# The up projection of two channel mixers: tokens stationary instead of weights, with the result turned back through 32x32 blocks and DRAM

## The chip, the cores and the metric

The kernel runs on one core of a Trainium2 chip. Five engines work side by side on it: TensorE (PE in the profile, its weight loads on a row of their own, PEld), VectorE (DVE), ScalarE (ACT), GpSimd (POOL) and SyncE (SP). Each takes its instructions strictly in the order of its own queue. Data moves between DRAM and the on-chip memory through 16 DMA engines that all queues share. Here SP issues nearly all transfers. The metric is device time in microseconds of one execution; the median of three runs stands for the kernel.

## The reference, cut to what matters

Two layers work on 256 tokens with 2048 features, all in float32. Layer 0 mixes tokens with gated linear attention, layer 1 with forgetting attention, and each also attends to 256 memory tokens. After each mixer comes a channel mixer, and this is where the change lies:

```python
def causal_dwconv(u, w, b):
    s_ = u.shape[1]
    up = jnp.pad(u, ((0, 0), (CONV_WIDTH - 1, 0), (0, 0)))
    return w[0] * up[:, 0:s_] + w[1] * up[:, 1:s_ + 1] + w[2] * up[:, 2:s_ + 2] + b

def conv_ffn(h, w_up, conv_w, conv_b, w_down):
    u = causal_dwconv(h @ w_up, conv_w, conv_b)
    a, val = split_cols(u, [FFN_HIDDEN, FFN_HIDDEN])
    return (jax.nn.silu(a) * val) @ w_down
```

`h` is the normalised residual (256 x 2048), `w_up` is 2048 x 11264 (a gate half and a value half of 5632 columns each), `w_down` is 5632 x 2048. The convolution runs along the tokens, with its own three weights and a bias for every hidden column.

## The kernel before

**Precision.** A float32 product is made from parts. Every activation and every weight is split into a rounded high part and the remainder (`hi`, `lo`), and a product is hi·hi + lo·hi + hi·lo. The weights stream from DRAM as units of 128 x 1024 values (512 KB, `raw`, four buffers). ScalarE rounds a unit to `whi` (L199, three buffers), VectorE subtracts to get `wlo` (L208, three buffers). So every unit passes SP, ScalarE and VectorE before TensorE can use it, and its `whi` buffer is free again when TensorE has used the unit up.

**Two forms of a projection.** `proj_fm` (L211 on) keeps a 128 x 128 block of weights stationary and streams the tokens. One matmul takes the weights' high part against both parts of the activations side by side (512 columns, L233 and L236), a second the weights' low part against the high part of the activations (256 columns, L234). The result has features on partitions and tokens along the row; the two halves of the 512 columns are added afterwards by `whole` (a copy on ScalarE, L241, and an addition on VectorE, L243). A unit holds four chunks of 128 input features by 256 output columns. `proj_tm` (L246 on) keeps 128 tokens stationary and streams 512 weight columns, three matmuls for each chunk of input features and each half of the tokens (L270, L271, L272). Its result has tokens on partitions. A unit holds two chunks by 512 columns.

**The channel mixer.** `ffn` (L780 on) goes through the hidden columns in three parts of 16, 16 and 12 blocks of 128 (`PARTS`). For each block `j` an up panel by `proj_fm` gives 128 gate columns and the 128 value columns that belong to them. Each result is put together by `whole`, multiplied by the norm's row of token factors into a tile `u` with two leading zeros (L795), convolved along the row (one ACTIVATE at L799, two VectorE operations at L800 and L801), and the pair of results goes through SiLU (L804), the product (L805) and `split` (L296, L297) into the tile of high and low parts that the down projection reads. After each part, four down panels by `proj_tm` add into the residual (L774). There are 44 up panels and 12 down panels in each layer. The first down panel of a part reads the part's blocks in order, two for each unit, so it needs the last two blocks only with its last unit: the eighth unit in a part of 16, the sixth in the part of 12.

**What sets the order of the work.** A planner (the tile scheduler) fixes each engine's queue at build time. It plays the program on a modelled machine and gives an engine, whenever that is free, the first in program order of the instructions whose inputs are there in the model; the weight stream (`split_unit`) has its place in that order moved ahead by 300. On the chip the queues then run in exactly that order, with semaphores for the dependencies. The accumulators in PSUM have four banks, and an up panel takes two of them, so a panel can be computed while the one before is read out.

The functions that the change touches, and what calls them:

Of the kernel before, what the change touches and what calls it, by code (L numbers as in the profile page):

```python
# [39 lines left out]

OG_EARLY = 2
# [13 lines left out]
def _panels():  # L55
# [79 lines left out]
M_N = M_LVL + NVER * len(LEVELS)  # L135
# [3 lines left out]
def _trunk(ctx: ExitStack, tc: tile.TileContext, xt, xtok, memt, wp, wgu, gns, gfin, cnv, par, msk, out):  # L139
# [12 lines left out]
    mask = const.tile([P, M_N], F32, name="mask")  # L152
# [15 lines left out]
    mk = [const.tile([P, MEM_H, T], F32, name=f"mk{l}") for l in range(2)]  # L168
    mv = [const.tile([P, 2, MEM_H * HD], F32, name=f"mv{l}") for l in range(2)]
# [76 lines left out]
    def proj_tm(key, src, evac, spare=None):  # L246

        units = where[key]  # L250
        n = units[0][2]
        base = min(min(u[1]) for u in units)
        acc = [pacc.tile([P, 512], F32, name="acc", tag="acc") for _ in range(2)]
        ahead = 0 if spare is None else 4
        ready = {}
        for i in range(len(units) + ahead):
            for b, u in ((0, i), (1, i - ahead)):
                if not 0 <= u < len(units):
                    continue
# [5 lines left out]
                xs = slice(b * P, (b + 1) * P)  # L265
                for j, kc in enumerate(kcs):
                    s = slice(j * n, (j + 1) * n)
                    xk = src[kc - base]
                    last = u == len(units) - 1 and j == len(kcs) - 1
                    TE.matmul(a, xk[:, 0, xs], hi[:, s], start=u == 0 and j == 0, stop=False)  # L270
                    TE.matmul(a, xk[:, 0, xs], lo[:, s], start=False, stop=False)  # L271
                    TE.matmul(a, xk[:, 1, xs], hi[:, s], start=False, stop=last)  # L272
                if u == len(units) - 1:
                    evac(b, a)
# [27 lines left out]
    class Norm:  # L302


        def __init__(self, n, tag="x"):
            self.n, self.tag = n, tag
            self.acc = self.y = self.r = None
# [53 lines left out]

    class StreamNorm(Norm):
# [49 lines left out]
    nx = StreamNorm()  # L412
    with tc.tile_pool(name="load", bufs=1) as lp:
# [55 lines left out]
        with tc.issue_after(loads[-1].ins):  # L469
            for i in range(KC):  # L470
                nc.sync.dma_start(xf[i], xt[i])
            nc.sync.dma_start(part, par)
            nc.sync.dma_start(mask[:, M_FOX:], msk[:, M_FOX:])
# [306 lines left out]
    def ffn(l, nx, h, m, then, spare=None):  # L780
        with tc.tile_pool(name=f"ffn{l}", bufs=1) as fp:
            cw = fp.tile([P, 4 * 88], F32, name="cw")
            nc.sync.dma_start(cw, cnv[l])
            us = [fp.tile([P, T + 2], F32, name=f"u{i}") for i in range(4)]
            for u in us:
                nc.gpsimd.memset(u[:, :2], 0.0)
            turn = [0]
            for p, (lo, hi) in enumerate(PARTS):
                for j in range(lo, hi):
                    cv = {}  # L790

                    def evac(c, a, j=j, cv=cv, i=j - lo):
                        u = us[turn[0] % 4]
                        turn[0] += 1
                        V.tensor_tensor(u[:, 2:], whole(a), nx.row(), ALU.mult)  # L795
# [3 lines left out]
                        S.activation(r, u[:, 2:], AF.Identity, bias=w[3], scale=w[2])  # L799
                        V.scalar_tensor_tensor(r, u[:, 1 : T + 1], w[1], r, ALU.mult, ALU.add)  # L800
                        V.scalar_tensor_tensor(r, u[:, :T], w[0], r, ALU.mult, ALU.add)  # L801
                        cv[c] = r
                        if c == 1:
                            S.activation(cv[0], cv[0], AF.Silu)  # L804
                            V.tensor_tensor(r, cv[0], r, ALU.mult)  # L805
                            split(m, i, r)

                    proj_fm(("up", l, j), h, evac)
# [27 lines left out]
    with tc.tile_pool(name="stash", bufs=1) as st:  # L836
# [11 lines left out]
        fox(n2, vt)  # L848
    n, then = preparing("ffn1", bufA)
# [37 lines left out]
def _constants():  # L887
# [5 lines left out]
    m[:, M_SCAN : M_SCAN + T] = np.where(np.arange(T) % 64 == 0, 0.0, 1.0)[None, :]  # L893
    for li, B in enumerate(LEVELS):
# [59 lines left out]
```

## Time and profile before

| | |
|---|---|
| median of three runs | 2302.28 us (2302.2 to 2302.3) |
| span of the profiled execution | 2300.7 us |
| TensorE busy | 2286.8 us, 99% |
| VectorE busy | 1614.6 us, 70% |
| ScalarE busy | 1252.9 us, 54% |
| granted TensorE clock | 0.999 |
| DRAM traffic | 187 GB/s over the span |

The profiled execution shows a span, from its first to its last instruction, of 2300.7 us, 1.6 us under the median of the runs; a sum that is made against the span carries over to the median with these 1.6 us added. A group's row in the profile gives the line, the engine, the operation, the tiles and shapes, the count, the busy time and the mean duration of one in ns, and then the engine's idle time before such instructions with what ended it. Matmuls are pipelined: the duration of one (389 ns for 512 columns) is longer than the time from one start to the next, so a rate has to be taken from a stretch of time divided by its count, and not from the mean duration. A window's row gives the busy time of each engine and its number of instructions in a stretch, then the granted clock, the busy share of the DMA engines, and GB/s.

### The profile page before, as it was taken

How to read it: one execution, taken by the hardware profiler on the slowest of the kernel's cores; microseconds unless marked ns; L12 is line 12 of the kernel's file. 1: busy time of each engine (PE TensorE's matmuls, PEld its weight loads, DVE VectorE, ACT ScalarE, POOL GpSimd, SP SyncE). 2: the span in 40 equal slices, each digit the busy share in tenths (PEclk: the TensorE clock that was granted, in tenths of full speed). 3: DMA queues.
4: the chain of work that ended last, by engine and by line, in shares of the span. 5: the costliest groups of instructions: out<-in, count | busy, mean ns of one | idle time of the engine just before them, and what ended most of it. 6: DMA issues, size and time to landing. Idle time of an engine off the chain costs nothing.

```text
span 2300.7 us, 33144 instructions
## 1 busy us (share of the span) xinstructions
PE 2286.8 (99%) x12392; PEld 1977.8 (86%) x12392; DVE 1614.6 (70%) x2639; ACT 1252.9 (54%) x1961; POOL 3.0 (0%) x19
## 2 busy tenths in 40 slices
PE   9999999999999999999999999999999999999998
PEld 7889888888888888888888998888888888888886
DVE  7568987577765777557767557657776577756775
ACT  7555565555553555445565555556554455534554
POOL 0000000000000000000000000000000000000000
PEclk9999999999999999999999999999999999999999
DMA  8644455555555555555555564555555555555554
GB/s 317 196 160 160 150 165 177 187 182 190 190 190 194 187 191 189 192 191 189 190 183 185 180 194 158 166 191 188 186 191 192 192 187 189 190 195 191 186 190 156
DMA packets 124745, 430.15 MB, mean 187 GB/s; under 512 B 14108, under 2 KB 18600, under 8 KB 124456
## 3 DMA queue, kind: packets, MB, share of 16 engines
q1 hardware_dynamic: 124152, 427.24, 55.7%
q8 instruction: 97, 1.59, 0.3%
q10 hardware_dynamic: 432, 0.79, 0.1%
q14 instruction: 64, 0.52, 0.1%
HBM read 425.87 MB, written 2.11 MB: 186 GB/s over the span
## 4 chain that ended last, share of the span: by engine, by line
PE 99%; DMA 0%; ACT 0%; DVE 0%; issue 0%; SPq 0%; DVEq 0%; ACTq 0%
PE acc L233 37%; PE acc L234 20%; PE acc L271 12%; PE acc L272 12%; PE acc L270 12%; PE acc L236 2%; PE ps_s L825 0%; PE ps_s L614 0%; PE ps_t L388 0%; PE ps_s L395 0%; PE ps_o L406 0%; DMA mt<-memt 0%; PE ps_s L739 0%; PE ps_o L633 0%; PE ps_o L755 0%; PE ps_s L533 0%
## 5 line engine op out<-in xcount | busy, mean ns | idle before, releaser
L208 DVE TENSOR_TENSOR wlo<-raw,whi 128x1024 fp32r<-128x1024 f32 (+4 forms) x812 | 972.7, 1199 | 547.3 <-ACT whi L199 533.3
L199 ACT ACTIVATE whi<-raw 128x1024 fp32r<-128x1024 f32 (+4 forms) x812 | 843.5, 1040 | 775.7 <-PE acc L272 370.6
L233 PE MATMUL acc<-B,whi 128*128 128x512 f32 x1980 | 684.1, 396 | 0.0
L233 PE MATMUL acc<-A,whi 128*128 128x512 f32 x1680 | 579.1, 396 | 1.9 <-DVE A L300 1.5
L234 PE MATMUL acc<-B,wlo 128*128 128x256 f32 x2112 | 551.2, 281 | 0.0
L234 PE MATMUL acc<-A,wlo 128*128 128x256 f32 x1792 | 463.9, 281 | 0.7 <-DVE wlo L208 0.7
L233 PEld LDWEIGHTS acc<-B,whi 128*128 128x128 f32 x1980 | 360.9, 188 | 69.0
L234 PEld LDWEIGHTS acc<-B,wlo 128*128 128x128 f32 x2112 | 397.7, 188 | 21.7
L234 PEld LDWEIGHTS acc<-A,wlo 128*128 128x128 f32 x1792 | 337.3, 188 | 21.6 <-DVE wlo L208 1.7
L233 PEld LDWEIGHTS acc<-A,whi 128*128 128x128 f32 x1680 | 304.9, 188 | 58.8 <-DVE A L300 1.9
L271 PE MATMUL acc<-wlo,B 128*128 128x512 f32 (+3 forms) x736 | 274.9, 374 | 1.2 <-DVE wlo L208 1.2
L272 PE MATMUL acc<-whi,B 128*128 128x512 f32 (+3 forms) x736 | 274.0, 373 | 0.0
L270 PE MATMUL acc<-whi,B 128*128 128x512 f32 (+3 forms) x736 | 247.6, 372 | 0.0
L271 PE MATMUL acc<-wlo,A 128*128 128x512 f32 x544 | 212.6, 391 | 0.0
L272 PE MATMUL acc<-whi,A 128*128 128x512 f32 x544 | 211.8, 389 | 0.0
L270 PE MATMUL acc<-whi,A 128*128 128x512 f32 x544 | 192.6, 391 | 0.0
L241 ACT ACTIVATE part<-acc 128x256 f32<-128x256 f32 x240 | 90.0, 375 | 163.1 <-PE acc L236 163.1
L271 PEld LDWEIGHTS acc<-wlo,B 128*128 128x128 f32 x736 | 138.2, 188 | 21.0 <-DVE wlo L208 1.6
L272 PEld LDWEIGHTS acc<-whi,B 128*128 128x128 f32 x736 | 138.3, 188 | 18.7
L270 PEld LDWEIGHTS acc<-whi,B 128*128 128x128 f32 x736 | 137.5, 188 | 18.7
L243 DVE TENSOR_TENSOR wholes<-acc,part 128x256 f32<-128x256 f32 x240 | 101.1, 421 | 66.3 <-ACT part L241 65.9
L272 PEld LDWEIGHTS acc<-whi,A 128*128 128x128 f32 x544 | 102.2, 188 | 21.2
(201 smaller groups left out, 1571.2 us busy)
## 6 DMA issues: line engine op xcount, KB each, us to landing
raw<-wp SPq DMA_DIRECT2D x743, 512.0 KB, 3.5
raw<-wp SPq DMA_DIRECT2D x32, 384.0 KB, 3.1
raw<-wp SPq DMA_DIRECT2D x24, 388.0 KB, 3.5
raw<-wp SPq DMA_DIRECT2D x8, 400.0 KB, 3.0
xf<-xt SPq DMA_DIRECT2D x16, 128.0 KB, 4.5
x<-xtok SPq DMA_DIRECT2D x4, 512.0 KB, 6.7
mt<-memt SPq DMA_DIRECT2D x3, 512.0 KB, 7.1
cb<-cdram SPq DMA_DIRECT2D x12, 128.0 KB, 3.3
```

Of the source, the lines that this page charges most:

```text
L199: casts.append(S.activation(hi[:, s], raw[:, s], AF.Copy))
L208: V.tensor_tensor(lo[:, s], raw[:, s], hi[:, s].bitcast(F32), ALU.subtract)
L233: TE.matmul(a, hi[:, s], both, start=done == 0, stop=False)
L234: TE.matmul(a[:, :T], lo[:, s], both[:, 0, :], start=False, stop=False)
L236: TE.matmul(a, hi[:, s], both, start=False, stop=True)
L241: S.activation(t, a[:, T:], AF.Copy)
L243: V.tensor_tensor(r, a[:, :T], t, ALU.add)
L270: TE.matmul(a, xk[:, 0, xs], hi[:, s], start=u == 0 and j == 0, stop=False)
L271: TE.matmul(a, xk[:, 0, xs], lo[:, s], start=False, stop=False)
L272: TE.matmul(a, xk[:, 1, xs], hi[:, s], start=False, stop=last)
```

## The change

The up panels of the channel mixers are taken in pairs. One panel now has four blocks of 128 columns (gate `j`, gate `j+1`, value `j`, value `j+1`) and is computed by `proj_tm`, with the tokens stationary. Half `b` of the tokens is every second token, starting at `b`, so that the stationary operand is read with a step of two.

The result (128 tokens x 512 columns, for each half) is copied by ScalarE with the token's norm factor as its scale, and VectorE turns it in blocks of 32 x 32 into one half of the tile `square`, every second element. The host has ordered the 512 columns by `SPREAD` so that, after this, partition `32 b + i` holds tokens `64 b` to `64 b + 63` in order, for 16 columns. One transfer writes `square` (512 KB, 4 KB a partition) to a DRAM tile, and four transfers read it back, one for each block of 128 columns, with four runs of 256 bytes for each partition. All five are issued from ScalarE's queue. From there, convolution, SiLU, product and `split` are as before; they stand one pair later in the program (`late`), except that the last pair of a part follows at once.

The norm's factors for the two interleaved halves are picked out of the row of factors once for each mixer (`mixed`), with two masks that are loaded with the mixer's other constants. `whole` and the multiplication by the row are no longer used in the up panels. The tiles of memory keys and values move from the constants to a pool that is closed after the forgetting attention. The core of the diff:

```diff
+SPREAD = [128 * q + 32 * k + i for k in range(4) for i in range(32) for q in range(4)]
...
+    def turned(key, w, blocks, kcs=full):
+
+        out.append((key, w, kcs, [(blocks, 512)], 2))
...
-            for j in range(lo, hi):
-                fm(("up", l, j), ("ffn_w_up", l), j * P, second=HID + j * P)
+            for j in range(lo, hi, 2):
+                turned(("up", l, j), ("ffn_w_up", l), [c + k * P for c in (0, HID) for k in (j, j + 1)])
...
-    def proj_tm(key, src, evac, spare=None):
+    def proj_tm(key, src, evac, spare=None, mixed=False):
...
-                    xk = src[kc - base]
+                    if mixed:
+                        xh, xl = (src[kc - base][:, i, b::2] for i in range(2))
+                    else:
+                        xh, xl = (src[kc - base][:, i, b * P : (b + 1) * P] for i in range(2))
                     last = u == len(units) - 1 and j == len(kcs) - 1
-                    TE.matmul(a, xk[:, 0, xs], hi[:, s], start=u == 0 and j == 0, stop=False)
-                    TE.matmul(a, xk[:, 0, xs], lo[:, s], start=False, stop=False)
-                    TE.matmul(a, xk[:, 1, xs], hi[:, s], start=False, stop=last)
+                    TE.matmul(a, xh, hi[:, s], start=u == 0 and j == 0, stop=False)
+                    TE.matmul(a, xh, lo[:, s], start=False, stop=False)
+                    TE.matmul(a, xl, hi[:, s], start=False, stop=last)
...
+        def mixed(self, picks):
+
+            if self.m is None:
+                row = self.row()
+                self.m = sm.tile([P, 2], F32, name="mixed", tag="mixed")
+                for h in range(2):
+                    pick = picks[:, h * T : (h + 1) * T]
+                    sq = sm.tile([P, T], F32, name="sq", tag="sq", bufs=2)
+                    V.tensor_tensor_reduce(sq, row, pick, 1.0, 0.0, ALU.mult, ALU.max, self.m[:, h : h + 1])
+            return self.m
...
-            us = [fp.tile([P, T + 2], F32, name=f"u{i}") for i in range(4)]
+            picks = fp.tile([P, 2 * T], F32, name="picks")
+            nc.sync.dma_start(picks, msk[:, M_PICK:])
+            us = [fp.tile([P, 4, T + 2], F32, name=f"u{i}") for i in range(3)]
...
-                    def evac(c, a, j=j, cv=cv, i=j - lo):
-                        u = us[turn[0] % 4]
-                        turn[0] += 1
-                        V.tensor_tensor(u[:, 2:], whole(a), nx.row(), ALU.mult)
-                        col = (c * 44 + j) * 4
+
+            def taken(j, base, u):
+
+                for i in range(2):
+                    cv = []
+                    for c in range(2):
+                        v = u[:, 2 * c + i, :]
+                        col = (c * 44 + j + i) * 4
                         w = [cw[:, col + n : col + n + 1] for n in range(4)]
                         r = fp.tile([P, T], F32, name=f"cv{c}", tag=f"cv{c}", bufs=3)
...
+                        S.activation(r, v[:, 2:], AF.Identity, bias=w[3], scale=w[2])
+                        V.scalar_tensor_tensor(r, v[:, 1 : T + 1], w[1], r, ALU.mult, ALU.add)
+                        V.scalar_tensor_tensor(r, v[:, :T], w[0], r, ALU.mult, ALU.add)
+                        cv.append(r)
+                    S.activation(cv[0], cv[0], AF.Silu)
+                    V.tensor_tensor(cv[1], cv[0], cv[1], ALU.mult)
+                    split(m, j + i - base, cv[1])
+
+            for p, (lo, hi) in enumerate(PARTS):
+                late = None
+                for j in range(lo, hi, 2):
+                    square = fp.tile([P, 16, 32, 2], F32, name="square", tag="square", bufs=2)
+
+                    def evac(b, a, square=square):
+                        e = fp.tile([P, 512], F32, name="scaled", tag="scaled", bufs=2)
+                        S.activation(e, a, AF.Copy, scale=nx.mixed(picks)[:, b : b + 1])
+                        V.transpose(square[:, :, :, b], e.rearrange("p (c t) -> p c t", t=32))
+
+                    proj_tm(("up", l, j), h, evac, mixed=True)
+                    d = dp.tile([4, 32, 4, 4, 64], F32, name="turned", tag="turned", bufs=3)
+                    nc.scalar.dma_start(d.rearrange("b i q k t -> (b i) (q k t)"), square.rearrange("p c t h -> p (c t h)"))
+                    u = us[turn[0] % 3]
+                    turn[0] += 1
+                    for k in range(4):
+                        nc.scalar.dma_start(u[:, k, 2:].rearrange("p (b t) -> p b t", b=4),
+                                          d[:, :, :, k, :].rearrange("b i q t -> (i q) b t"))
+                    if late is not None:
+                        taken(*late)
+                    late = (j, lo, u)
+                taken(*late)
                 end = p == len(PARTS) - 1
                 add_out(("down", l, p), m, then if end else None, spare if end else None)
```

More of the change, by code (lines that the diff above doesn't have):

```diff
@@ L306, in __init__ @@
             self.n, self.tag = n, tag
-            self.acc = self.y = self.r = None
+            self.acc = self.y = self.r = self.m = None
         def add(self, src):
@@ L412, in _trunk @@
     nx = StreamNorm()
+    memory = ctx.enter_context(ExitStack())
+    mp = memory.enter_context(tc.tile_pool(name="memory", bufs=1))
+    mk = [mp.tile([P, MEM_H, T], F32, name=f"mk{l}") for l in range(2)]
+    mv = [mp.tile([P, 2, MEM_H * HD], F32, name=f"mv{l}") for l in range(2)]
     with tc.tile_pool(name="load", bufs=1) as lp:
@@ L848, in _trunk @@
         fox(n2, vt)
+    memory.close()
     n, then = preparing("ffn1", bufA)
@@ L893, in _constants @@
     m[:, M_SCAN : M_SCAN + T] = np.where(np.arange(T) % 64 == 0, 0.0, 1.0)[None, :]
+    for h in range(2):
+        m[r, M_PICK + h * T + 2 * r + h] = 1.0
     for li, B in enumerate(LEVELS):
```

36 lines of the change are left out of this document (15 added, 21 removed).

## The prediction

> **What bounds the kernel now.** I read the page first, then a table of stretches cut at the borders between up and down panels, then the groups of one stretch, then single instructions. The page's span, its row for TensorE and the chain that ended last:
>
> ```profile
> span 2300.7 us, 33144 instructions
> ...
> PE 2286.8 (99%) x12392; PEld 1977.8 (86%) x12392; DVE 1614.6 (70%) x2639; ACT 1252.9 (54%) x1961; POOL 3.0 (0%) x19
> ...
> PE 99%; DMA 0%; ACT 0%; DVE 0%; issue 0%; SPq 0%; DVEq 0%; ACTq 0%
> ```
>
> TensorE is the bound from end to end and nothing holds it up. So a change is worth what it takes off TensorE's own stream, less every moment for which it makes TensorE wait. The table of stretches (up part, down part, up part, then the last up parts, of 12 panels, of layer 0 and of layer 1):
>
> ```profile
> core 0: us, PE busy (x) PEld busy (x) DVE busy (x) ACT busy (x) POOL busy (x), PEclk, DMA share, GB/s
> 745.60:924.30 178.70, 178.70 (x1025) 156.01 (x1024) 138.47 (x216) 102.61 (x155) 0.00 (x0) 1.00 0.57 189
> 924.30:1011.40 87.10, 87.10 (x385) 72.09 (x385) 46.94 (x49) 36.21 (x38) 0.00 (x0) 1.00 0.57 193
> 1011.40:1145.50 134.10, 134.10 (x770) 117.03 (x769) 103.09 (x160) 76.47 (x115) 0.00 (x0) 1.00 0.57 189
> 2092.20:2226.30 134.10, 134.10 (x769) 117.01 (x769) 103.14 (x160) 76.46 (x115) 0.00 (x0) 1.00 0.56 189
> ```
>
> TensorE is busy in the whole of each, at the full clock. An up part of 16 panels takes 178.7 us, so two panels take 178.7 / 8 = 22.34 us. A down part is four panels of the very form that the change gives to the up panels: 16 chunks, two halves, three matmuls of 512 columns, 96 matmuls. It takes 87.1 us, so 21.78 us a panel, or 226.8 ns a matmul.
>
> **TensorE's term.** One new panel replaces two old ones. Both stream the same columns: old 2 x 16 x 2 x (512 + 256) = 49152, new 96 x 512 = 49152. What differs is the number of matmuls, 128 against 96. The rows say 22.34 against 21.78 us, 0.56 us a pair, and there are 44 pairs in the two layers: 44 x 0.5625 = **24.8 us** less. It breaks even at 22.34 / 96 = 232.7 ns a matmul, only 5.9 ns above the row.
>
> The Trainium skill speaks against even this. TensorE: Matmul & The Clock Gate, section "Wait — 56ns, not 53.3ns?", gives a fixed cost of about 2.5 ns a matmul beyond its columns; by it 32 matmuls fewer would save 0.08 us a pair, an estimate of 3.5 us in all. The trace disagrees: its two forms differ by 0.56 us.
>
> One thing in the new panels differs from the down panels: the stationary operand is read with a step of two. No row shows a strided weight load. The nearest rows are loads of 128 and of 64 columns:
>
> ```profile
> L272 PEld LDWEIGHTS acc<-whi,A 128*128 128x128 f32 x544 | 102.2, 188 | 21.2
> ...
> L614 PEld LDWEIGHTS ps_s<-gdd,ks 128*64 128x64 f32 x128 | 6.0, 137 | 1.7 <-issue 1.5 <-ACT whi L199 0.2
> ```
>
> 64 columns more cost 51 ns, so 128 columns take about 102 ns of reading, which hides behind a matmul of 226.8 ns. If the step doubled it, 204 ns would still hide; at four times, 408 ns, it would set the pace. I take no change; the far ends are 0 and 408 - 227 = 181 ns a matmul.
>
> **VectorE and ScalarE in a pair.** The groups of the stretch 745.6 to 924.3 us:
>
> ```profile
> L208 DVE TENSOR_TENSOR wlo<-raw,whi 128x1024 fp32r<-128x1024 f32 x64 | 78.5, 1226 | 28.3 <-ACT whi L199 26.5
> L199 ACT ACTIVATE whi<-raw 128x1024 fp32r<-128x1024 f32 x64 | 67.9, 1061 | 54.5 <-PE acc L233 26.0 <-ACT cv L804 13.9 <-ACT cv L799 12.7
> L799 ACT ACTIVATE cv<-u,cw 128x256 f32<-128x256 f32 x30 | 17.7, 591 | 0.0
> L801 DVE SCALAR_TENSOR_TENSOR cv<-u,cw,cv 128x256 f32<-128x256 f32 x30 | 14.4, 482 | 0.5
> ...
> L795 DVE TENSOR_TENSOR u<-wholes,row 128x256 f32<-128x256 f32 x30 | 12.7, 423 | 0.5
> L243 DVE TENSOR_TENSOR wholes<-acc,part 128x256 f32<-128x256 f32 x30 | 12.6, 421 | 9.0 <-ACT part L241 9.0
> ...
> L241 ACT ACTIVATE part<-acc 128x256 f32<-128x256 f32 x31 | 11.6, 375 | 23.1 <-PE acc L236 23.1
> L805 DVE TENSOR_TENSOR cv<-cv,cv 128x256 f32<-128x256 f32 x15 | 6.4, 425 | 1.6
> ...
> L296 ACT ACTIVATE A<-cv 128x256 fp32r<-128x256 f32 x15 | 6.3, 417 | 0.0
> L804 ACT ACTIVATE cv<-cv 128x256 f32<-128x256 f32 x15 | 6.0, 402 | 0.0
> ```
>
> VectorE loses four additions (L243) and four multiplications (L795), 4 x (421 + 423) = 3.38 us a pair. It gains two turns of 128 x 512. No row shows a turn. Its ends are an operation of 128 x 512 at 0.68 us (the row of L774, below) and the 1.23 us of a subtraction over twice as many elements (L208); I take 0.68, the row of its own size, hence 1.36 us a pair. The rest stays: 8 subtractions 9.8 us, 8 convolution steps of 0.48 us, and 2 products and 2 splits of 0.42 us, 5.5 us. Together 16.7 of 21.8 us, 77%, as today (138.47 of 178.70); at 1.23 us a turn 82%. Not the bound.
>
> ScalarE loses four copies (L241), 1.50 us, and gains two scaled copies of 128 x 512 at 0.67 us (L450) and five issues of transfers. For these:
>
> ```profile
> L774 DVE TENSOR_TENSOR x<-x,acc 128x512 f32<-128x512 f32 x64 | 41.2, 681 | 4.8 <-PE acc L272 4.8
> ...
> L450 ACT ACTIVATE mv<-acc,ny 128x512 f32<-128x512 f32 x4 | 2.7, 674 | 0.7 <-PE acc L272 0.7
> ...
> L882 ACTq DMA_DIRECT2D out<-x x2: 338/346/354, 2291.4 to 2296.0; - x2
> ...
> L732 SPq DMA_DIRECT2D cb<-cdram x12: 319/327/428, 1310.8 to 1443.0; - x12
> ...
> L728 SPq DMA_DIRECT2D cdram<-fc x1: 372/372/372, 1309.5 to 1309.5; - x1
> ```
>
> An issue from ScalarE takes 0.35 us. A transfer of 12 rows (L728) takes as long to issue as one of 128 rows (L732), so I price the reads' 512 runs at 0.35 us too; the upper end is four times, 1.4 us. Five make 1.7 us. ScalarE's sum: 8 x 1.06 + 1.35 + 4 x 0.59 + 2 x (0.40 + 0.42) + 1.7 = 15.5 us of 21.8, 71% (57% today); at the upper end 19.7 us, 91%.
>
> Per mixer there are two reductions for `mixed` and a mask load from SP ahead of the first read-out. I cost them at nothing: two of the four accumulator banks are free, and the next pair keeps TensorE busy for 21.8 us. Without that cover they would cost about 1 us a mixer. The moved memory tiles issue nothing.
>
> **The DMA engines.** The rows of the queues, and of transfers to landing:
>
> ```profile
> q1 hardware_dynamic: 124152, 427.24, 55.7%
> ...
> q10 hardware_dynamic: 432, 0.79, 0.1%
> ...
> raw<-wp SPq DMA_DIRECT2D x743, 512.0 KB, 3.5
> ...
> cb<-cdram SPq DMA_DIRECT2D x12, 128.0 KB, 3.3
> ...
> out<-x ACTq DMA_DIRECT2D x2, 256.0 KB, 2.5
> ```
>
> q1 moves 427 MB in 55.7% of 2300.7 us on 16 engines, so 512 KB cost 1.57 us of all 16. A pair's eight units cost 12.6 us, and its write 1.6 us. The reads are 2048 runs of 256 bytes, 128 for each engine, and no row shows such packets. At q1's rate by bytes they cost 1.6 us. At the price of a packet on q10 (0.1% x 2300.7 x 16 / 432 = 85 ns, for 1.8 KB) they cost 10.9 us. I take twice the rate by bytes, 25 ns a run, so 3.2 us: a run is far nearer to a seventh of q10's packets than to a whole one. That makes 17.4 of 21.8 us, 80%. The units have room for this: four `raw` buffers are nearly four units, 10.9 us, ahead of their need, and land in 3.5.
>
> **Where TensorE could wait, in the steady state.** A `whi` buffer comes free when TensorE has used a unit up; the cast follows at once, then the subtraction. In a down part:
>
> ```profile
> 962.67 1.06 ACT L199 ACTIVATE whi<-raw 128x1024 fp32r<-128x1024 f32 x1 [1.66 <-PE acc L272]
> ...
> 963.76 1.23 DVE L208 TENSOR_TENSOR wlo<-raw,whi 128x1024 fp32r<-128x1024 f32 x1 [1.50 <-ACT whi L199]
> ...
> 965.39 1.06 ACT L199 ACTIVATE whi<-raw 128x1024 fp32r<-128x1024 f32 x1 [1.66 <-PE acc L272]
> ```
>
> A unit lasts 965.39 - 962.67 = 2.72 us. The unit cast at 962.67 is wanted two units later, at 968.11, and is ready at 964.99. So ScalarE and VectorE together may be 3.1 us late before TensorE stands. What the change can put ahead of a cast: the four reads in a row, 4 x 0.35 = 1.4 us, and one running operation on each engine, 0.67 and 0.68 us. Together 2.7 us, under 3.1. I cost the steady state at **0**, as long as the planner puts the reads behind what is ready before the write has landed.
>
> **Where TensorE will wait: the ends of parts.** After a part's last up matmul (E) the down panel starts at once, and wants the last two blocks with its last unit: at E + 7 x 2.72 = 19.0 us in a part of 16 blocks, at E + 5 x 2.72 = 13.6 us in the part of 12, the second block 0.7 us later. The chain to them, from the rows above: read-out of half 1 (0.3 wait + 0.67), turn (half a subtraction, 0.6, + 0.68), so E + 2.3. The write: a load of the same size takes 3.5 us to land, a write of half of it 2.5; I take 3.3 and 0.5 for a cast ahead of it: E + 6.1. Third read issued 0.7 later, landing in 3.3 plus 1.0 for the many runs: E + 11.1; the fourth E + 11.5. Then convolution of the value block (0.59 + 2 x 0.48), product 0.43, rounding 0.42, with 1.5 us of waits behind casts and subtractions: first block E + 15.0, second E + 17.2. The parts of 16 have 2.5 us left. The part of 12 is late by 17.2 - 14.3 = 2.9 us, once in each layer: **5.8 us**. Without any wait it is about 0; its upper end is in the rivals. Late next would be the write.
>
> **The sum.** Profiled execution: 2300.7 - 24.8 + 5.8 = 2281.7 us span; the median stands 1.6 us higher: 2302.3 - 24.8 + 5.8 = **2283 us**, 0.8% faster.
>
> **The rivals.**
>
> *ScalarE stands at the reads (slower).* ScalarE's queue is strict, and the first read cannot issue before the write has landed. If the planner's model lands the write too early, the casts behind the reads wait for the landing too: 3.3 + 1.4 = 4.7 us against 3.1 allowed, 1.6 us a pair, 44 x 1.6 = 70 us: 2353 us. It decides the sign from (24.8 - 5.8) / 44 = 0.43 us a pair on, a hold of 3.5 us. For it: casts every 2.7 us, and reads whose runs may issue slower. Against: before the change VectorE and ScalarE queues with many such crossings never stop TensorE.
>
> *DMA engines become the bound (slower).* From (21.8 - 14.2) us / 128 = 59 ns a run on, the reads fill what the units leave. At 85 ns a pair takes 25.1 us of the DMA engines: 3.3 us more, 145 us, 2428 us with the same part ends. For it: q10's row. Against: the runs are a seventh of q10's packets. The Trainium skill, DMA: Bandwidth & Descriptors, section "Specifications", puts the least transfer for full rate at 512 bytes, below which the engine reads, modifies and writes; it gives no time, and no row here shows a run of 256 bytes.
>
> *Strided weight loads set the pace (slower).* With the part ends counted, 19.0 us over 4224 matmuls, it decides from 4.5 ns a matmul on; at 10 ns more, 4224 x 10 ns = 42 us: 2325 us. For it: the margin is small. Against: twice the reading time still fits.
>
> *The gain is spent at the ends of parts (no change).* With 4.2 us more in each chain, the six ends cost 2 x 7.1 + 4 x 1.7 = 21 us: 2299 us. For it: the chain has two passes through DRAM. Against: engines have a quarter of their time free.
>
> **How the numbers follow.** Forecast 0.52; ScalarE stands 0.22; strided loads 0.08; DMA bound 0.07; spent at the ends 0.11. About 0.2% (4.6 us) is what a measurement tells from no change. Faster is the forecast and its near cases, 0.53; same 0.11; slower 0.36. The forecast's own range is 2276 (nothing at the ends, a little better pace) to 2297. The whole range goes up to 2335, which takes in the end case, half of the stands and most strided cases; what is left out is about 0.2.
>
> **What would show it.** TensorE: 226.8 ns a matmul in an up part, 174.2 us for 16 blocks. A turn near 0.68 us, an issue near 0.35 us, reads landing under 5 us, DMA share near 0.8. TensorE's idle only before the last unit of the first down panel of a part of 12. The forecast is wrong if idle of TensorE stands before L270 to L272 in every pair with a late cast ahead of it, if ScalarE's own wait is a read's issue, or if the pace of the up matmuls is over 232 ns with no idle at all.

## The result and the profile after

The changed kernel takes 2335.48 us (median of four runs, 2332.28 to 2341.57) against 2302.29 us beside it: a ratio of 1.0147, interval 1.0133 to 1.0162. It is 1.5% slower. The prediction said 2283 us, faster, with a range up to 2335: the sign is wrong. The page of the profiled run (2332.28 us): span, busy time by engine, and the chain that ended last.

```profile
span 2330.5 us, 30207 instructions
...
PE 2302.4 (99%) x10984; PEld 1933.3 (83%) x10984; DVE 1517.8 (65%) x2383; ACT 1243.5 (53%) x1873; POOL 2.9 (0%) x17
...
PE 85%; DMA 9%; DVE 2%; ACT 2%; issue 1%; ACTq 0%; SPq 0%; DVEq 0%
```

TensorE's share of the chain fell from 99% to 85%, and 9% is now DMA. The table of stretches says where: an up part of 16 blocks and its down part, the up part of 12 of layer 0 and its down part, the last down part.

```profile
core 0: us, PE busy (x) PEld busy (x) DVE busy (x) ACT busy (x) POOL busy (x), PEclk, DMA share, GB/s
...
750.70:931.70 181.00, 180.47 (x769) 147.73 (x768) 118.22 (x164) 99.34 (x135) 0.00 (x0) 1.00 0.70 224
931.70:1019.40 87.70, 87.41 (x386) 72.05 (x385) 49.39 (x54) 37.67 (x42) 0.00 (x0) 1.00 0.65 209
1019.40:1158.00 138.60, 135.99 (x577) 110.93 (x576) 86.96 (x120) 73.87 (x99) 0.00 (x0) 1.00 0.68 217
1158.00:1229.40 71.40, 68.56 (x313) 56.26 (x312) 48.59 (x68) 45.78 (x87) 0.31 (x1) 1.00 0.60 199
...
2250.80:2330.50 79.70, 67.93 (x289) 54.87 (x287) 47.79 (x73) 36.79 (x70) 0.00 (x0) 0.93 0.53 172
```

Cut the same way, the kernel before had 178.7, 87.1, 134.1, 68.1 and 74.4 us there. Over both layers the six up parts went from 985.7 to 1003.7 us and the six down parts from 490.8 to 502.4; the rest stayed (824.2, 824.4). So +18.0 and +11.6 make up nearly all of the 29.8 us by which the span grew. The profiled execution is the fastest of the four; the median grew by 33.2 us. The up parts should have lost 24.8.

Two things are new in an up part. The first is in its groups (columns: busy us, mean ns of one, idle before and what ended it), and in a row from the groups of the down part behind it:

```profile
L279 PEld LDWEIGHTS acc<-whi,B 128*128 128x128 f32 x256 | 49.4, 193 | 10.0
...
L825 ACT ACTIVATE cv<-u,cw 128x256 f32<-128x256 f32 x28 | 16.2, 599 | 9.5 <-DMA u<-turned 9.5
...
L841 DVE STREAM_TRANSPOSE square<-scaled 128x512 f32<-128x512 f32 x14 | 9.9, 707 | 0.0
```

```profile
L279 PEld LDWEIGHTS acc<-whi,A 128*128 128x128 f32 x128 | 24.0, 188 | 4.9
```

A strided weight load takes 193 ns against 188: far below a matmul, as forecast. But the matmuls start every 233 ns in the up parts and every 227 ns in the down parts. At 96 matmuls a pair that is 22.40 us, more than the 22.34 of the two old panels. The second is ScalarE's timeline in one pair (start, duration; in brackets its idle time before and what ended it):

```profile
799.62 0.34 ACTq L845 DMA_DIRECT2D turned<-square  x1
802.24 1.06 ACT L204 ACTIVATE whi<-raw 128x1024 fp32r<-128x1024 f32 x1 [1.79 <-PE acc L279]
804.91 1.48 ACTq L849 DMA_DIRECT2D u<-turned  x3
806.52 1.06 ACT L204 ACTIVATE whi<-raw 128x1024 fp32r<-128x1024 f32 x1 [3.22 <-issue]
806.54 0.42 ACTq L849 DMA_DIRECT2D u<-turned  x1
809.63 1.66 ACT L825 ACTIVATE cv<-u,cw 128x256 f32<-128x256 f32 x3 [2.05 <-DMA u<-turned]
811.19 1.05 ACT L204 ACTIVATE whi<-raw 128x1024 fp32r<-128x1024 f32 x1
```

The first read stands at the head of ScalarE's queue until the write has landed (5.3 us after its issue), and three reads take 1.48 us to issue. So the cast due at 805.0, a unit of 2.80 us after the one at 802.24, runs at 806.5. Then the convolutions of the pair just read stand there until the reads have landed, and the cast behind them, due at 807.8, waits until 811.2. It is 3.4 us late, and TensorE loses 0.1 us by it. In the pair before, the cast at the same place was due at 784.6, two units after the one at 778.96. It is 4.2 us late, and TensorE waits; with the slower matmuls around the gap this costs 0.9 us:

```profile
788.78 1.05 ACT L204 ACTIVATE whi<-raw 128x1024 fp32r<-128x1024 f32 x1
...
791.16 0.50 PE L278 MATMUL acc<-wlo,B 128*128 128x512 f32 x1 [0.54 <-DVE wlo L213]
```

The convolutions' results are wanted only in the down part; the planner put them that early. The transfers (packets, MB and share of a queue; then KB and median us to landing; then the reads' issues, ns, least, median and most):

```profile
q1 hardware_dynamic: 124440, 427.77, 55.8%
q10 hardware_dynamic: 99696, 46.95, 7.2%
...
raw<-wp SPq DMA_DIRECT2D x743, 512.0 KB, 3.8
turned<-square ACTq DMA_DIRECT2D x44, 512.0 KB, 5.9
u<-turned ACTq DMA_DIRECT2D x176, 128.0 KB, 4.1
```

```profile
L849 ACTq DMA_DIRECT2D u<-turned x176: 366/528/1569, 510.4 to 2261.7; - x176
```

The write lands in 5.9 us, not the 3.3 of the prediction, and a read takes 0.53 us to issue, not 0.35. The Trainium skill, Perfetto Trace Analysis, section "DMA Instruction — HWDGE (DVE, Sync)", says that a transfer's semaphore waits until its writes are confirmed, and that this can be surprisingly long into HBM; a load of the same size into the core's own memory lands in 3.8 us here, so the rows agree, though no run separates this cause from others.

### The profile page after: what moved, and what is told of

It reads as the page before. It is cut to its first block, busy times and chain, and to the rows that moved or that the text cites. A ratio compares the mean times of both kernels' runs of the same rounds, so it can differ in the third digit from the quotient of the medians.

```text
span 2330.5 us, 30207 instructions
## 1 busy us (share of the span) xinstructions
PE 2302.4 (99%) x10984; PEld 1933.3 (83%) x10984; DVE 1517.8 (65%) x2383; ACT 1243.5 (53%) x1873; POOL 2.9 (0%) x17
## 4 chain that ended last, share of the span: by engine, by line
PE 85%; DMA 9%; DVE 2%; ACT 2%; issue 1%; ACTq 0%; SPq 0%; DVEq 0%
PE acc L278 22%; PE acc L279 22%; PE acc L277 21%; PE acc L238 10%; PE acc L239 5%; DMA turned<-square 5%; DMA u<-turned 3%; DVE wlo L213 1%; ACT whi L204 1%; ACT cv L825 1%; PE acc L241 1%; DMA raw<-wp 1%; DVE cv L826 0%; PE ps_s L871 0%; ACTq L849 0%
## 5 line engine op out<-in xcount | busy, mean ns | idle before, releaser
L213 DVE TENSOR_TENSOR wlo<-raw,whi 128x1024 fp32r<-128x1024 f32 (+4 forms) x812 | 971.5, 1198 | 691.6 <-ACT whi L204 685.5
L278 PE MATMUL acc<-wlo,B 128*128 128x512 f32 (+3 forms) x1440 | 554.5, 386 | 5.9 <-DVE wlo L213 5.9
L279 PE MATMUL acc<-whi,B 128*128 128x512 f32 (+3 forms) x1440 | 551.1, 384 | 0.0
L277 PE MATMUL acc<-whi,B 128*128 128x512 f32 (+3 forms) x1440 | 497.8, 384 | 3.7 <-ACT whi L204 3.5
L278 PE MATMUL acc<-wlo,A 128*128 128x512 f32 x1248 | 491.7, 395 | 3.2 <-DVE wlo L213 2.7
L279 PE MATMUL acc<-whi,A 128*128 128x512 f32 x1248 | 488.1, 392 | 0.0
L277 PE MATMUL acc<-whi,A 128*128 128x512 f32 x1248 | 441.3, 393 | 2.2 <-ACT whi L204 2.2
L278 PEld LDWEIGHTS acc<-wlo,B 128*128 128x128 f32 x1440 | 274.6, 191 | 61.1 <-DVE wlo L213 14.1
L277 PEld LDWEIGHTS acc<-whi,B 128*128 128x128 f32 x1440 | 273.7, 191 | 52.4 <-ACT whi L204 5.6
L279 PEld LDWEIGHTS acc<-whi,B 128*128 128x128 f32 x1440 | 274.8, 191 | 46.1
L277 PEld LDWEIGHTS acc<-whi,A 128*128 128x128 f32 x1248 | 237.8, 191 | 52.1 <-ACT whi L204 2.9
L279 PEld LDWEIGHTS acc<-whi,A 128*128 128x128 f32 x1248 | 238.2, 191 | 48.4
L238 PE MATMUL acc<-B,whi 128*128 128x512 f32 x660 | 232.7, 397 | 0.0
L239 PE MATMUL acc<-B,wlo 128*128 128x256 f32 x704 | 192.4, 284 | 0.0
L238 PE MATMUL acc<-A,whi 128*128 128x512 f32 x360 | 127.8, 399 | 1.9 <-DVE A L307 1.1
L239 PE MATMUL acc<-A,wlo 128*128 128x256 f32 x384 | 105.1, 288 | 0.7 <-DVE wlo L213 0.7
```

The source lines that it names most:

```text
L213: V.tensor_tensor(lo[:, s], raw[:, s], hi[:, s].bitcast(F32), ALU.subtract)
L238: TE.matmul(a, hi[:, s], both, start=done == 0, stop=False)
L239: TE.matmul(a[:, :T], lo[:, s], both[:, 0, :], start=False, stop=False)
L277: TE.matmul(a, xh, hi[:, s], start=u == 0 and j == 0, stop=False)
L278: TE.matmul(a, xh, lo[:, s], start=False, stop=False)
L279: TE.matmul(a, xl, hi[:, s], start=False, stop=last)
```

## The experiments

In all of them the kernel before took 2302.0 to 2302.3 us beside it. The first theory (S): two causes, the stride (233 against 227 ns a matmul) and the hold on ScalarE. Rivals: the stride only seems to cost (C), or the trip costs by its traffic (B).

**Contiguous weight loads alone.** The tokens of a half are the first or the last 128, so values land on wrong tokens; all else is the same.

```
- xh, xl = (src[kc - base][:, i, b::2] for i in range(2))
+ xh, xl = (src[kc - base][:, i, b * P : (b + 1) * P] for i in range(2))
```

> Left as the changed kernel in every instruction and in every queue's order, but each half of the tokens is read as 128 tokens side by side, step one, in place of every second token (the tokens then land in the wrong places of the result, so this times the step alone). Theory S (the stride): the step of two costs the 6.3 ns by which an up matmul (233.3 ns from start to start) lags a down matmul (227.0); without it the up matmuls run at 227.0 ns, 4224 x 6.3 ns = 27 us less, 2335 -> about 2308 us, and the waits of TensorE stay. Rival C (the transfers): the up parts are slower because 256-byte reads and the write share the memory with TensorE; then the pace stays at 233 ns and the time at 2335 us.

Measured: 2323.18 us (2318.03 to 2326.3), ratio 1.0095 (1.0079 to 1.0112). The matmuls start every 227 ns, and a weight load takes 188 ns:

```profile
L279 PEld LDWEIGHTS acc<-whi,B 128*128 128x128 f32 x205 | 38.5, 188 | 7.8
```

The stride is the whole of the 6.3 ns. But 4224 matmuls by 6.3 ns are 26.6 us, and only 12 came back. At the faster pace the up parts take 960.2 us with nothing held (the first run on the end of a part, below); here they took 991.2. TensorE's stands there (the times in which it waits) doubled, from 15.4 us (1003.7 less the 988.3 of the next run but one) to 31.0. A unit now lasts 2.72 us and not 2.80, so each cast is due earlier while the hold keeps its length; that this is how they doubled is argued, not measured by itself.

**A step of four.** Every fourth element of the two stacked operands, so the products are of the wrong numbers.

```
- xh, xl = (src[kc - base][:, i, b::2] for i in range(2))
+ xh, xl = (src[kc - base].rearrange("p i t -> p (i t)")[:, 2 * i + b :: 4] for i in range(2))
```

> The changed kernel with the stationary operand read with a step of four (over the high and low parts as one row of 512, so the result means nothing); instructions and orders unchanged. If the cost of the stride grows with the distance spanned, the pace goes from 227.0 (step one) over 233.3 (step two) to about 246 ns, 4224 x 12.6 ns = 53 us more, about 2388 us. If it has its jump where reading the weights no longer hides behind a matmul, a step of four takes 400 ns and more, some 700 us more. If the stride is not the cause of the slow pace, nothing changes: 2335 us.

Measured: 2349.49 us, a single execution. The load takes 310 ns, but the matmuls start 235 ns apart:

```profile
L279 PEld LDWEIGHTS acc<-whi,B 128*128 128x128 f32 x202 | 62.5, 310 | 0.0
```

Neither law of the expectation holds. A load 122 ns longer, and longer than the time between two matmuls, moves the pace by 8 ns; one 5 ns longer by 6.3. So the price of the stride isn't the load's duration; what it is stays open.

**No trip through DRAM.** The turned tile goes straight to the convolutions, at their sizes; the write and the reads are left out, so blocks are put together wrongly.

```
- d = dp.tile([4, 32, 4, 4, 64], F32, name="turned", tag="turned", bufs=3)
- nc.scalar.dma_start(d..., square...)
- for k in range(4): nc.scalar.dma_start(u[:, k, 2:]..., d[:, :, :, k, :]...)
```

> The changed kernel without the write and the four reads: the convolution reads the turned tile itself, 256 columns at a time (values in the wrong places; the transfers through DRAM are left out). Theory S+L (stride and landings): the waits of TensorE come from ScalarE standing at the landings of the write and the reads, so they go, and the pace of 233.3 ns stays: span of before 2301 + 2.5 us for the pace = 2303, time 2303 to 2309 us. Rival C: without transfers the pace falls to 227 ns too: about 2280 us. Rival B (the engines are simply fuller): the waits stay, 2325 us or more.

Measured: 2305.52 us (2305.09 to 2306.06), ratio 1.0014 (1.0005 to 1.0023). An up part and the down part behind it:

```profile
746.10:925.30 179.20, 179.20 (x770) 148.22 (x769) 119.32 (x165) 101.03 (x135) 0.00 (x0) 1.00 0.58 188
925.30:1012.30 87.00, 87.00 (x385) 72.08 (x384) 48.38 (x53) 37.86 (x41) 0.00 (x0) 1.00 0.61 194
```

No idle moment of TensorE: 179.20 us / 768 = 233.3 ns a matmul. The up parts are 988.3 us, 2.6 over before, and the down parts 491.2. So the stride alone ends 0.14% over before, and the trip costs the other 27 us by the profiled executions (2330.5 less 2303.9), 30 us by the medians.

**Transfers kept, their landing not waited for.** The convolutions read a constant tile, so the blocks are constants.

```
- v = u[:, 2 * c + i, :]
+ v = still
```

> The changed kernel with all transfers, but the convolution reads a constant tile, so nothing waits for the four reads to land (the data path through DRAM ends in an unread tile). Theory L2 (the second landing): the hold that stops TensorE is the convolution at the head of ScalarE's queue waiting for the reads, 3 us and more on top of the reads' own 2 us of issue; without it TensorE's waits go almost wholly, 2304 to 2312 us. Rival L1 (the first landing): the hold is the first read waiting for the write; then most of the waits stay, 2320 us or more. Rival D (the load on the DMA engines delays the weights): the waits stay, 2330 us.

Measured: 2326.14 us (2325.32 to 2329.05), ratio 1.0106 (1.0091 to 1.0121), so the total missed. In the steady parts TensorE has no gap at all, with all the traffic there (178.7 us for 766 matmuls), which speaks for the landing and against B. The 2326 comes from the start of each mixer: freed convolutions ran ahead of the norm's small operations, and the first up part took 189.2 and 190.2 us. An artefact of the edit, so the next run takes the wait away in another way.

**Convolutions queued behind a later cast.** Theory L2: it is the convolutions' place that costs; L1: the first read's.

```
- taken(*late)
+ with tc.issue_after(casts[-1].ins):
+     taken(*late)
```

> The changed kernel with its convolutions held back: on ScalarE's queue those of a pair stand behind the last cast of the next pair's weights (an order alone, nothing is left out). Theory L2 (ScalarE stands at the landing of the reads): by then the reads have landed, the casts ahead are no longer late, and TensorE's waits go; the pace stays 233.3 ns: 2303 to 2310 us. Rival L1 (it stands at the first read, until the write has landed): that wait is untouched, 2320 us or more.

Measured: 2321.09 us (2318.48 to 2322.26), ratio 1.008 (1.0065 to 1.0095). By its total that is the number of L1. The stretches tell more (up, down, last down):

```profile
747.10:926.30 179.20, 179.20 (x770) 148.22 (x769) 117.39 (x162) 99.89 (x134) 0.00 (x0) 1.00 0.73 228
926.30:1014.60 88.30, 87.80 (x386) 71.88 (x385) 49.39 (x56) 38.17 (x43) 0.00 (x0) 1.00 0.65 206
...
2237.20:2318.70 81.50, 69.16 (x289) 55.75 (x287) 47.91 (x75) 37.41 (x71) 0.00 (x0) 0.92 0.52 165
```

In the up parts every stand is gone, 988.3 us as with no trip, although the reads still go out from ScalarE ahead of casts (two of them at 1621.03, and the cast behind them found its engine idle for 2.47 us, where 1.7 is usual): L2 there. All that is left is in the down parts, 506.6 us against 490.8, behind the last pair of a part, whose convolutions this edit doesn't hold.

**Tokens sorted beforehand.** The norm stores even tokens first, so the loads are contiguous and the values right.

```
- xh, xl = (src[kc - base][:, i, b::2] for i in range(2))
+ xh, xl = (src[kc - base][:, i, b * P : (b + 1) * P] for i in range(2))
+ hi, lo = (t.rearrange("p (h t) -> p t h", h=2) for t in (hi, lo))   # in split, for the mixer's operand
+ src = src.rearrange("p (t h) -> p t h", h=2)
```

> The changed kernel, but the tile of normalised activations is stored with the even tokens first and the odd tokens after them, so that the matmuls read a half with step one and the result is as wanted; the waits are untouched. Theory S: pace 227.0 ns, and, as with the contiguous halves, the faster pace leaves less time for the casts, so 2318 to 2326 us. Rival: writing the activations apart is slow on ScalarE and VectorE, 2330 us or more.

Measured: 2323.97 us (2322.19 to 2327.46), ratio 1.0096 (1.0081 to 1.0111), as expected and as with contiguous loads: the order can be had for nothing that the time shows.

**Both.**

> Both of the above. If stride and landings are all that stood between the forecast and the measurement, nothing of the 24.8 us is lost: 2276 to 2284 us, faster than the kernel before by about 1%. If a third cause is there (DMA engines, fuller queues, ends of parts), 2290 us or more.

Measured: 2290.83 us (2289.77 to 2293.11), ratio 0.9952 (0.9936 to 0.9969): faster than before, and 7 to 15 us over the expectation. Up and down:

```profile
742.10:916.20 174.10, 174.10 (x770) 144.16 (x769) 116.79 (x161) 99.65 (x134) 0.00 (x0) 1.00 0.76 234
916.20:1004.40 88.20, 87.70 (x385) 71.79 (x384) 49.54 (x57) 38.16 (x43) 0.00 (x0) 1.00 0.67 206
```

174.10 us / 768 = 226.7 ns: the up parts sum to 961.0 us, 24.7 less than before, the prediction's 24.8. The down parts, 502.9, keep 12.1 too much.

**Transfers from GpSimd's queue.** The write and the four reads are issued there, with nothing else changed. It asks whether the issues on ScalarE cost.

```
- nc.scalar.dma_start(...)   (the write and the reads)
+ nc.gpsimd.dma_start(...)
```

> The changed kernel with its five transfers a pair issued from GpSimd's queue, which is empty; ScalarE then neither spends 2 us a pair on issuing nor stands at the write, but the convolutions still stand at the reads. Theory L2: most of the waits stay, 2322 to 2335 us. Rival I (the issues and the first read's wait on ScalarE are the hold): 2303 to 2312 us.

Measured: 2371.06 us (2363.42 to 2374.55), ratio 1.0294 (1.0275 to 1.0313), outside both expectations. ScalarE's wait for the reads (us, times, longest), after the change and here, and the reads' issues here:

```profile
ACT cv L825 <- DMA u<-turned: 63.7, 46, 3.1
```

```profile
ACT cv L825 <- DMA u<-turned: 240.6, 57, 7.0
```

```profile
L849 POOL DMA_DIRECT2D u<-turned x176: 749/749/763, 510.6 to 2306.0; - x176
```

GpSimd takes 0.75 us a read, so the last one goes out 0.9 us later and lands later (4.7 us after its issue in the median, against 4.1), and the convolutions stand at ScalarE's head for longer. Whatever ScalarE gained by issuing nothing was lost in this longer wait.

**The same with both remedies.**

> held_sorted with the write and the four reads of each pair issued by GpSimd's queue (0.56 us and 4 x 0.75 us there in the run of pool, against 0.34 and 4 x 0.53 us on ScalarE's). Pool alone was slower than the changed kernel, 2371 us, and ScalarE's wait of its convolutions for the reads grew from 63.7 to 240.6 us. Theory L (what cost time in pool is only that wait: convolutions at the head of ScalarE's queue, with the casts behind them): with the convolutions queued behind the next panel's last cast the wait is gone, the six up parts sum to 960-963 us as in held_sorted, and as ScalarE no longer stands at the first read of a part's last pair, the down parts are at most 503: 2282-2292 us. Theory G (transfers from GpSimd's queue cost TensorE time in themselves, by slower landings of the weights or by slower VectorE operations): the up parts show gaps again or the weights land later, and the time is 2300 us or more.

Measured: 2341.9 us (2337.17 to 2347.9), ratio 1.0171 (1.0149 to 1.0192). The number is theory G's, but the trace shows the wait of theory L:

```profile
ACT cv L828 <- DMA u<-turned: 123.4, 81, 5.4
```

From the write's issue to the last landing it takes 14.1 us here in the median over the pairs (15.2 at most), against 11.4 us (13.4) in the run of both remedies, so the one cast behind which the convolutions are queued is now too early a place. Neither of theory G's causes is in the trace: 512 KB of weights land in 4.0 us in the median here and in 4.2 us there, and a subtraction (L213) takes 1197 ns here and 1198 ns there.

**The end of a part.** Three runs, each with both remedies, ask what the 12.1 us are. In the first, the last pair's reads are queued behind a cast of the down panel and its convolutions behind that panel's last cast.

```
+ if behind is not None and u in behind:          # in proj_tm, after a unit's cast
+     with tc.issue_after(casts[-1].ins):
+         behind[u]()
...
- taken(*late)
+ behind = {last - 2 if last > 6 else last - 1: read, last: lambda late=late: taken(*late)}
```

> held_sorted with the end of each part written out too: the last pair's four reads are queued behind a cast of the first down panel (its unit 5 of 8, its unit 4 of 6) and its convolutions behind that panel's last cast. In held_sorted the six up parts sum to 961.1 us (985.7 in the kernel before, so -24.6), while the six down parts sum to 502.9 against 490.8, +12.1. Theory E (ScalarE's queue stands there at the first read, which waits for the write, and at the convolutions, which wait for the reads, and the casts of the first down panel come late): the down parts fall to 491-496 us and the time to 2279-2284 us. Theory B (the chain of the last pair through DRAM is too long, and TensorE waits for its blocks whoever stands where; the prediction's end of parts): the down parts stay at 498 us or more, the time at 2286 us or more, and the gaps are ended by the rounding of a block instead of a cast.

Measured: 2294.13 us (2288.37 to 2295.74), ratio 0.9957 (0.994 to 0.9974). Neither theory's case: the down parts rose to 509.1 us, yet casts and subtractions end the gaps, not blocks. ScalarE there:

```profile
926.37 2.05 ACTq L857 DMA_DIRECT2D u<-turned  x4
928.54 1.06 ACT L204 ACTIVATE whi<-raw 128x1024 fp32r<-128x1024 f32 x1 [2.51 <-PE acc L282]
930.36 1.06 ACT L204 ACTIVATE whi<-raw 128x1024 fp32r<-128x1024 f32 x1 [0.76 <-PE acc L282]
932.91 0.60 ACT L831 ACTIVATE cv<-u,cw 128x256 f32<-128x256 f32 x1 [1.49 <-DMA u<-turned]
```

The reads still take 2 us of the queue, and the first convolution, which waits for them, starts 6.5 us after they begin to go out. In the second, the last pair's reads go out from SP; nothing else differs from both remedies.

```
+ queue = nc.sync if j + 2 == hi else nc.scalar
- nc.scalar.dma_start(u[:, k, 2:]..., d[:, :, :, k, :]...)
+ queue.dma_start(u[:, k, 2:]..., d[:, :, :, k, :]...)
```

> held_sorted, and the four reads of each part's last pair are issued by SP in place of ScalarE; all else stays. In held_sorted the six down parts are 502.9 us against 490.8 before. In its part of 12 one cast started at 1145.86 where it could have at about 1144.1, behind the first read's wait for the write, and the next at 1149.23, behind convolutions that waited for the reads. Theory R (the stand at the first read is at least half of the 12.1 us): the down parts fall to 497 us or less, 2279-2286 us. Theory C (the convolutions' stand for the reads is the larger half): the down parts stay at 499-503 us, 2286-2292 us. If SP, standing at the reads, delays the weights' loads, the down parts rise and the time is over 2293 us.

Measured: **2282.08 us** (2280.8 to 2284.24), ratio 0.9915 (0.9898 to 0.9931). Up, down, and the down parts of the two parts of 12:

```profile
741.10:915.20 174.10, 174.10 (x769) 144.19 (x768) 116.72 (x161) 99.58 (x134) 0.00 (x0) 1.00 0.75 234
915.20:1002.30 87.10, 87.10 (x385) 72.02 (x384) 49.68 (x57) 38.19 (x43) 0.00 (x0) 1.00 0.65 209
1133.50:1203.30 69.80, 68.64 (x313) 56.16 (x312) 49.17 (x71) 46.47 (x89) 0.31 (x1) 1.00 0.63 202
2203.20:2279.10 75.90, 66.08 (x289) 53.70 (x287) 48.19 (x76) 37.55 (x71) 0.00 (x0) 0.96 0.57 178
```

Theory R holds: the down parts fall to 494.0 us, so 8.9 of the 12.1 us came with those reads in ScalarE's queue, which stood at them and issued them. The convolutions' own stand for reads is no shorter than with both remedies alone (17.0 us in all against 11.0), which speaks against theory C. In the parts of 16 nothing is left; the parts of 12 keep 1.7 and 1.5 us. The third also queues the last convolutions behind the first down panel's last cast.

> ends_sp, and the convolutions of each part's last pair are queued behind the last cast of the first down panel (in ends_sp they stand behind the second or third cast after the write). Theory R and theory C both: neither the first read nor, in the parts of 16, the convolutions hold a cast, so the down parts are 493-497 us, 2277-2283 us, and the gaps left are those of the two parts of 12, whose reads land when the last cast is already due. If four convolutions in a row delay the casts behind them by themselves (about 2.4 us on ScalarE and 3.9 us on VectorE with nothing between), as in ends, the down parts stay at 500 us or more, 2287 us or more.

Measured: 2284.18 us (2282.87 to 2284.52), ratio 0.992 (0.9906 to 0.9935). The down parts are 497.1 us, 3.1 worse, between its two cases: four convolutions in a row delay a subtraction in each part of 16 by some 0.6 us (812 to 816 ns between two matmuls in place of 227, ended by L213).

## Why the prediction was wrong

- **TensorE's term: the step that failed first.** It took the down panel's 226.8 ns and "no change" for the step of two. With the step a matmul takes 233.3 ns, over the 232.7 at which the term breaks even: +2.6 us in the up parts in place of -24.8. The reasoning looked at whether a longer load still hides. It does, even at 310 ns, and the pace moved all the same. Of the strided rival the threshold held (it decides from 4.5 ns a matmul on, and the step costs 6.3), not its reason, a load too long to hide. The Trainium skill, SBUF — State Buffer, section "Specifications (TRN2)", asks for two hits in each line of 16 bytes for full bandwidth. By it a step of two f32 would keep full bandwidth and one of four would not: the loads agree (188, 193, 310 ns), the matmuls' pace (227, 233, 235 ns) does not.
- **Steady state at 0: the step that failed second.** 15.4 us of stands in the up parts. The allowance of 3.1 us was right (a cast 3.4 us late cost TensorE 0.1 us, one 4.2 us late 0.9), and its condition named the danger, but it counted only the reads' issues. What stood was the consumer: convolutions placed on ScalarE ahead of casts before their data had landed. The rival that came nearest put the stand at the first read, with 70 us; in the up parts, with the convolutions held and the reads left in place, it was 0.
- **Ends of parts, 5.8 us.** The down parts cost 11.6 us more. The forecast's mechanism (TensorE waits for the last blocks) isn't what the trace of the changed kernel shows: the planner let units of the second down panel go ahead of the late blocks (the first panel of a part of 16 is read out 24.6 us after the part's start, where it was 21.6), and late casts and subtractions ended the gaps. With both remedies the mechanism is there, but in the parts of 16, where the forecast had 2.5 us to spare, and not in those of 12. Each of the four has one wait of 0.5 us for the rounding of a block (L306); the rows of the two layers (us, times, longest):

```profile
PE acc L277 <- ACT A L306: 1.0, 2, 0.5
PE acc L277 <- ACT B L306: 1.0, 2, 0.5
```

With the last reads on SP these waits are gone. ScalarE's stand at the last reads was the larger cause; without it 3.2 us remain, in the parts of 12 only, behind a late cast and late subtractions.
- **The sum.** 2.6 + 15.4 + 11.6 + 0.2 elsewhere = 29.8 us, the span's growth.
- **Sizes that held.** The turn 0.71 us (0.68 forecast), the write's issue 0.34, a read's landing 4.1 us (4.3). The runs of 256 bytes were cheaper than 25 ns: q10 took 7.2% of 16 x 2330.5 us, 2685 us; its 23.1 MB of writes at q1's 48.6 us a MB take 1120 of them and the 432 packets of before 37, which leaves, as an estimate, 17 ns for each of 90112 runs. The records of these packets in the trace give 18.8 ns in the mean; at q1's rate by bytes it would be 12.4. The DMA share was 0.70, not 0.80, VectorE's 65% (77%). Too low were the write's landing (5.9 us for 3.3) and a read's issue (0.53 us for 0.35).
- **What the forecast described** does exist: with tokens sorted, convolutions held and the last reads on SP, the up parts lose 24.9 us, the down parts gain 3.2, and the kernel takes 2282.08 us. The 2283 was the time of a schedule that the change did not make. That 2282.08 lies so near it is in part luck: the up parts' gain is the forecast's term, but what remains at the ends is late casts and subtractions, not the wait for blocks that gave its 5.8 us.

## What to carry to other kernels

Price an operand's stride by the pace of the matmuls in a run that has it, not by whether its load still fits. In a strict queue every instruction that reads a transfer's result holds all behind it until the landing: ask of each consumer, not only of each issue, what stands behind it, and place it after work that is due sooner. A gain in pace shortens the time in which the other engines must deliver, so it can come back as waits until those are moved (here some 15 of 26.6 us did, and none in the up parts once the convolutions were moved).

## What the runs showed of the hardware beyond that

The step of the stationary operand moves load and pace apart: 188, 193, 310 ns a load and 227, 233, 235 ns a matmul at steps of 1, 2 and 4.

A short stop can cost more than itself. In the run with held convolutions TensorE stood 0.93 and 0.77 us within 2.5 us; the three stretches are that, what came next, and after:

```profile
1163.00:1165.50 2.50, 1.07 (x3) 0.59 (x4) 2.50 (x6) 2.50 (x6) 0.00 (x0) 0.99 0.54 175
1165.60:1168.90 3.30, 3.30 (x9) 2.59 (x8) 2.92 (x6) 0.76 (x1) 0.00 (x0) 0.51 0.53 165
1169.00:1172.00 3.00, 3.00 (x15) 2.47 (x14) 1.57 (x3) 1.67 (x3) 0.00 (x0) 1.00 0.51 161
```

For 3.3 us the granted clock was 0.51, with matmuls 427 ns apart: nine of them, some 1.7 us more lost. The length of the stop alone doesn't decide it. In the changed kernel TensorE stood 2.21 and 0.63 us from 1171.8 us on, and the clock stayed full; it stood 2.08 and 0.64 us from 2264.6 on, and half the clock followed. The stretches after the two:

```profile
1175.70:1179.00 3.30, 3.30 (x16) 2.73 (x15) 2.93 (x6) 1.71 (x4) 0.00 (x0) 1.00 0.56 197
...
2268.90:2272.30 3.40, 3.40 (x10) 2.67 (x9) 2.43 (x5) 0.52 (x2) 0.00 (x0) 0.52 0.79 229
```

The run with GpSimd's queue and both remedies has seven such stretches, 25.2 us at a clock of 0.50, each behind waits of TensorE, so some 12 us of its time are an after-effect of them. The Trainium skill, TensorE: Matmul & The Clock Gate, section "What's actually happening", tells of two clocks, full and half, switched by a free-running window of about 3.4 us; the half clock and its length agree, though in the run with held convolutions it came after 1.7 us of standing still in all.
